# Loading the SSD's skip weights as whole rows instead of single strided values

## The chip, the cores and the metric

The kernel runs on one core of a Trainium2 chip. The metric is the time of one execution on the device in microseconds (us), and smaller is better.

## The reference, cut to what matters

The kernel computes one layer of a diffusion backbone on 512 latent tokens and 256 context tokens of width 1024: an input projection, two mixing branches (RWKV-7 and Mamba-2 SSD), a merge, and an expert-choice mixture of experts. The change concerns one small parameter of the SSD branch, `ssm_d`, with one value for each of its 32 heads. It weighs the skip path, in which a head's input is added to its output:

```python
SSM_DIM = 2 * D_MODEL        # 2048
SSM_HEAD = 64                # channels of a head
SSM_HEADS = SSM_DIM // SSM_HEAD     # 32

def ssm_readout(y, q, p):
    b_, n = y.shape[:2]
    y = (y + p['ssm_d'].astype(F32)[:, None] * q['x'].astype(F32)).reshape(b_, n, SSM_DIM)
    return rms_norm(y * jax.nn.silu(q['z'].astype(F32)), p['ssm_norm'])
```

The 2048 channels are held in 16 blocks of 128, so a block of 128 partitions holds two heads: the even one in partitions 0 to 63 and the odd one in partitions 64 to 127.

## The kernel before, in words

The kernel holds one program order for each engine. TensorE's order is written out by hand in nearly all stages (`manual_schedule`); in the stage of the change the orders of VectorE, ScalarE, GpSimd and the DMA-issuing queues are laid out at build time by a planner (`schedule_with_timeline_sim`), which estimates when each instruction is due. At run time each engine works strictly in its order.

The stages are: norms and the first projections (to 110 us), preparation of the RWKV scan woven with projections, the scan itself (from some 690 to 1100 us, four head groups `p`), the SSD (to some 1530 us), merge, routing, and the experts.

In the scan, `scan` runs twelve steps for each `p`, each a short chain of small matmuls (line 902) and copies out of PSUM: into `R` (line 930), into `SV` by VectorE (944) and by ScalarE (945), and a product (954). Between the steps `feed` lets TensorE work through blocks of the input projection (lines 312 and 315). Such a block needs its weights: a load `wraw` of 0.5 MB on SyncE's queue (line 281), a rounding `whi` on ScalarE (284), and the rest `wlo` on GpSimd (287). Its result is copied out by ScalarE into `u` (453, 454), goes through a convolution on VectorE and ScalarE (459 to 466), and GpSimd's queue stores it (468, 469). Two more things run beside the scan: the late modulation weights, with loads `adaw` of 1 MB each on SyncE's queue (157) and short rows `aext` (1549, 1550), and the scan's own loads `sAL`, `sTT`, `sBT`, `sRT`, `sRB`, `SV` of 128 to 512 KB on SyncE's queue (880 to 892).

After the scan of `p` = 1, `ssd_setup` is entered. It builds constants on VectorE (`identR`, `sel`, `neg`, lines 1011 to 1022), loads `dpar`, and computes the step sizes `dt` from a load `dt` (1034) and two loads `dtprm` (1036, 1037): the first step of that is VectorE's line 1042, then ScalarE's 1043 and 1044, and some thirty instructions on VectorE follow. Its instructions are interleaved with the scan's by the planner.

`dpar` is a tile of 128 partitions by 16: column B holds, for block B, the even head's weight in partitions 0 to 63 and the odd head's in 64 to 127. It is filled by two DMAs from GpSimd's queue (line 1025), one for each half. Each repeats one row of the source over 64 partitions (step 0) and takes 16 values with a step of two. It is read 16 times, in `ssd_out` (line 1253), where VectorE computes `xk * dpar + y`.

`ssd_setup` gets the pool `sp` for what the SSD keeps (`dpar` too) and the pool `sc2`, as `p`, for what it needs for itself. `sc2` is closed at the end of the scan's stage.

Of the kernel before, what the change touches and what calls it, by code (L numbers as in the profile page):

```python
# [8 lines left out]
F32 = mybir.dt.float32  # L9
# [78 lines left out]
class Block:  # L88
# [916 lines left out]
    def ssd_setup(self, sp, p, ps):  # L1005


        nc, A = self.nc, self.A
# [12 lines left out]
                nc.vector.tensor_scalar(self.neg[:, d, c], jp, 0.0, -30000.0, op0=op, op1=OP.mult)  # L1021
        nc.vector.memset(self.ones, 1.0)
        self.dpar = sp.tile([128, 16], F32, name="dpar")
        for h in range(2):
            nc.gpsimd.dma_start(self.dpar[64 * h:64 * h + 64, :],
                                bass.AP(tensor=A["ssm_d"].tensor, offset=A["ssm_d"].offset + h, ap=[[0, 64], [2, 16]]))
        self.CH = sp.tile([128, SEQ], F32R, name="CH")
        self.ecumT = sp.tile([128, 4, 64], F32, name="ecumT")
        self.dtT = sp.tile([128, 4, 64], F32, name="dtT")
# [1076 lines left out]
```

## Time and profile before

| | us |
|---|---|
| median of 3 runs | 2210.12 |
| lowest and highest run | 2207.89, 2210.43 |
| profiled execution, its own time | 2214.4 |
| profiled execution, its span | 2212.3 |

The busy shares over the span are 87% for TensorE's matmuls, 53% for VectorE, 38% for ScalarE and 29% for GpSimd. The HBM traffic is 222 GB/s over the span.

Times in the rows are microseconds from the span's start, unless marked ns. PE is TensorE, PEld its weight loads, DVE VectorE, ACT ScalarE, POOL GpSimd, SP SyncE; a q behind an engine's name means its queue of DMA issues. `L1025` is line 1025 of the kernel, and `out<-in` are the program's names. What stands in square brackets behind an instruction is the idle time of its engine just before it and what ended that. The granted TensorE clock (PEclk) is a share of full speed.

### The profile page before, as it was taken

How to read it: one execution, taken by the hardware profiler on the slowest of the kernel's cores; microseconds unless marked ns; L12 is line 12 of the kernel's file. 1: busy time of each engine (PE TensorE's matmuls, PEld its weight loads, DVE VectorE, ACT ScalarE, POOL GpSimd, SP SyncE). 2: the span in 40 equal slices, each digit the busy share in tenths (PEclk: the TensorE clock that was granted, in tenths of full speed). 3: DMA queues.
4: the chain of work that ended last, by engine and by line, in shares of the span. 5: the costliest groups of instructions: out<-in, count | busy, mean ns of one | idle time of the engine just before them, and what ended most of it. 6: DMA issues, size and time to landing. Idle time of an engine off the chain costs nothing. (4 is left out here: it accounts for less than half of the span.)

```text
span 2212.3 us, 35294 instructions
## 1 busy us (share of the span) xinstructions
PE 1929.1 (87%) x13996; PEld 1276.1 (58%) x14016; DVE 1176.1 (53%) x1939; ACT 846.7 (38%) x1422; POOL 631.3 (29%) x484
## 2 busy tenths in 40 slices
PE   4979888798868857999997999789999998999997
PEld 2756666566646645666675666457888453433332
DVE  4355987887894829444443466674355112322214
ACT  5444554555443323343445345444334222111113
POOL 2244342523242222232333475664211000000002
PEclk8989988989988989999999999899999998999999
DMA  6246668767889686977555344336857898999997
GB/s 233 74 116 145 164 158 192 151 173 158 193 180 240 187 170 185 292 253 218 164 157 175 99 152 140 106 133 209 300 201 274 333 366 317 409 409 409 409 409 301
DMA packets 444655, 495.15 MB, mean 224 GB/s; under 512 B 138441, under 2 KB 339391, under 8 KB 441419
## 3 DMA queue, kind: packets, MB, share of 16 engines
q1 hardware_dynamic: 419755, 449.27, 64.2%
q0 software_dynamic: 7872, 26.75, 4.2%
q10 hardware_dynamic: 16864, 16.88, 2.4%
q8 instruction: 110, 1.80, 0.3%
q14 instruction: 54, 0.44, 0.1%
HBM read 393.95 MB, written 97.98 MB: 222 GB/s over the span
## 5 line engine op out<-in xcount | busy, mean ns | idle before, releaser
L287 POOL TENSOR_TENSOR wlo<-wraw,whi 128x1024 fp32r<-128x1024 f32 x92 | 231.4, 2515 | 505.1 <-ACT whi L284 205.9
L312 PE MATMUL pl<-hlH,whi 128*128 128x512 f32 x672 | 242.2, 438 | 17.8 <-DVE hlH L257 5.9
L312 PE MATMUL pl<-hlH,wlo 128*128 128x512 f32 x672 | 239.8, 435 | 0.0
L312 PE MATMUL pl<-hlL,whi 128*128 128x512 f32 x672 | 233.7, 428 | 0.0
L1703 PE MATMUL ph<-ew,xe 128*64 128x512 f32 x432 | 196.0, 596 | 0.8 <-DMA ew<-in_exp_w_dram 0.8
L1702 PE MATMUL ph<-ew,xe 128*64 128x512 f32 x432 | 195.5, 596 | 0.0
L284 ACT ACTIVATE whi<-wraw 128x1024 fp32r<-128x1024 f32 x93 | 98.1, 1055 | 243.7 <-DMA wraw<-in_w_in_dram 160.4
L312 PEld LDWEIGHTS pl<-hlH,whi 128*128 128x128 f32 x672 | 130.0, 198 | 61.5 <-issue 15.5
L312 PEld LDWEIGHTS pl<-hlH,wlo 128*128 128x128 f32 x672 | 129.0, 198 | 38.9 <-issue 14.1
L312 PEld LDWEIGHTS pl<-hlL,whi 128*128 128x128 f32 x672 | 127.6, 195 | 39.9 <-issue 14.2
L1702 PEld LDWEIGHTS ph<-ew,xe 128*64 128x64 f32 x432 | 56.5, 137 | 109.0 <-issue 107.5
L463 DVE SCALAR_TENSOR_TENSOR cacc<-u,cst,cacc 128x772 f32<-128x772 f32 (+1 forms) x96 | 98.4, 1025 | 33.3 <-ACT cacc L459 31.7
L315 PE MATMUL pc<-hcH,whi 128*128 128x256 f32 (+1 forms) x312 | 97.1, 312 | 20.0 <-ACT u L454 14.6
L1789 PE MATMUL pye<-ew,ewx 128*64 128x512 f32 x448 | 109.9, 642 | 0.0
L315 PE MATMUL pc<-hcL,whi 128*128 128x256 f32 (+1 forms) x312 | 95.9, 311 | 0.0
L315 PE MATMUL pc<-hcH,wlo 128*128 128x256 f32 (+1 forms) x312 | 94.9, 307 | 0.0
L1212 ACT ACTIVATE M<-sel,ncumT 128x128 f32<-128x128 f32 x256 | 69.3, 387 | 67.0 <-PE sel L1209 66.9
L1709 ACT ACTIVATE ewx<-ph 128x512 f32<-128x512 f32 x30 | 17.9, 598 | 184.3 <-PE ph L1703 171.6
L1817 DVE TENSOR_TENSOR macc<-macc,psc 128x512 f32<-128x512 f32 x56 | 37.7, 685 | 89.9 <-PE psc L1812 89.8
L1213 DVE TENSOR_TENSOR M<-M,cb 128x512 f32<-128x512 f32 x64 | 63.4, 999 | 35.0 <-ACT M L1212 34.8
L466 POOL TENSOR_TENSOR cacc<-cacc,csg 128x772 f32<-128x772 f32 (+1 forms) x24 | 42.4, 1765 | 135.2 <-ACT csg L465 134.6
L315 PEld LDWEIGHTS pc<-hcH,whi 128*128 128x128 f32 (+1 forms) x312 | 61.6, 197 | 30.2 <-ACT u L454 17.8
(574 smaller groups left out, 4228.2 us busy)
## 6 DMA issues: line engine op xcount, KB each, us to landing
ew<-in_exp_w_dram SPq DMA_DIRECT2D x126, 1024.0 KB, 16.6
ew<-in_exp_w_dram SPq DMA_DIRECT2D x90, 512.0 KB, 13.1
wraw<-in_w_in_dram SPq DMA_DIRECT2D x83, 512.0 KB, 4.1
adaw<-in_ada_w_dram SPq DMA_DIRECT2D x24, 1024.0 KB, 13.7
cst<-in_exp_w_dram SPq DMA_DIRECT2D x14, 1024.0 KB, 18.0
BTd<-BT ACTq DMA_DIRECT2D x48, 256.0 KB, 4.0
sAL<-ALd SPq DMA_DIRECT2D x23, 512.0 KB, 3.8
sBT<-BTd SPq DMA_DIRECT2D x23, 512.0 KB, 6.2
```

The source lines that it names most:

```text
L284: pin(nc.scalar.activation(hi, raw, AF.Copy))
L287: self.lo.tensor_sub(lo, raw, hi.bitcast(F32))
L312: nc.tensor.matmul(pl[:n], w_[:, kt, :n], x[0][:, kt, :], **e)
L315: nc.tensor.matmul(pc[:n], w_[:, kt, :n], x[1][:, kt, :], **e)
L463: e.scalar_tensor_tensor(acc[:, s0:s0 + n0], u[:, s0 + k:s0 + k + n0], cw[:, b, k:k + 1], acc[:, s0:s0 + n0], op0=OP.mult, op1=OP.add)
L466: nc.gpsimd.tensor_mul(acc[:, s:s + n], acc[:, s:s + n], sg[:, s:s + n])
L1212: nc.scalar.activation(M[:, c], pt[:, c * 128:c * 128 + 128], AF.Exp, bias=self.ncumT[:, c, r:r + 1])
L1213: nc.vector.tensor_mul(M.rearrange("p c t -> p (c t)"), M.rearrange("p c t -> p (c t)"), cb)
L1702: nc.tensor.matmul(ph[e][f][0:64], x, w1[j][:, fs], start=kt == 0, stop=kt == 7, skip_group_check=True)
L1703: nc.tensor.matmul(ph[e][f][64:128], x, w3[j][:, fs], start=kt == 0, stop=kt == 7, skip_group_check=True)
L1789: nc.tensor.matmul(py[64 * c:64 * c + 64], hd[e][:, kt], w2[j][:, 512 * c:512 * c + 512], start=kt == 0, stop=kt == 7, skip_group_check=True)
L1817: nc.vector.tensor_add(a, a, pc)
```

## The change

The two DMAs on GpSimd's queue go. In their place one DMA on SyncE's queue loads the whole row of 32 weights into each of the 128 partitions of a new tile `dall` (the source row is repeated with a step of 0, and each partition gets 32 neighbouring values, 128 bytes). Two VectorE copies then pick the even columns for partitions 0 to 63 and the odd columns for partitions 64 to 127 into `dpar`. `dall` takes 128 bytes of each partition in the pool `sc2`.

```diff
         self.dpar = sp.tile([128, 16], F32, name="dpar")
+
+        dall = p.tile([128, 32], F32, name="dall")
+        nc.sync.dma_start(dall, bass.AP(tensor=A["ssm_d"].tensor, offset=A["ssm_d"].offset, ap=[[0, 128], [1, 32]]))
         for h in range(2):
-            nc.gpsimd.dma_start(self.dpar[64 * h:64 * h + 64, :],
-                                bass.AP(tensor=A["ssm_d"].tensor, offset=A["ssm_d"].offset + h, ap=[[0, 64], [2, 16]]))
+            nc.vector.tensor_copy(self.dpar[64 * h:64 * h + 64, :], dall[64 * h:64 * h + 64, h::2])
         self.CH = sp.tile([128, SEQ], F32R, name="CH")
```

## Rows read from the trace of the kernel before

**Rows 1.** The page: TensorE's busy tenths in 40 equal slices of the span.

```profile
PE   4979888798868857999997999789999998999997
```

**Rows 2.** Stretches: length, busy us (instructions) of each engine, granted clock, DMA share, GB/s.

```profile
799.50:812.30 12.80, 0.00 (x0) 0.00 (x0) 0.00 (x0) 0.00 (x0) 0.00 (x0) 0.69 0.88 75
...
825.00:832.00 7.00, 7.00 (x60) 5.48 (x61) 6.96 (x7) 1.27 (x3) 0.28 (x1) 0.52 0.56 159
```

**Rows 3.** The tile `dpar`: durations ns min/median/max, first and last start; time to landing.

```profile
L1253 DVE SCALAR_TENSOR_TENSOR y<-xk,dpar,sy x16: 734/748/749, 1275.3 to 1520.2; 128x512 f32<-128x512 f32 x16
L1025 POOL DMA_DIRECT2D dpar<-in_ssm_d_dram x2: 829/846/864, 786.6 to 787.5; - x2
...
DMA to landing us min/median/max: 14.6/19.7/24.9
```

**Rows 4.** DMA, 789 to 793 us: flow in 40 slices; GpSimd's queue: packets, MB, share.

```profile
GB/s 328 492 246 573 164 246 573 410 246 328 655 328 328 655 118 77 533 241 256 282 348 274 251 207 184 120 56 41 54 46 38 20 8 0 0 0 0 0 0 0
...
q0 software_dynamic: 16, 0.00, 204.4%
```

**Rows 5.** DMA, 799 to 803 us: GpSimd's queue, columns as above.

```profile
q0 software_dynamic: 29, 0.00, 233.1%
```

**Rows 6.** Stretches of 2 us, columns as in rows 2.

```profile
788.00:790.00 2.00, 1.52 (x9) 1.07 (x8) 2.00 (x10) 0.00 (x0) 0.31 (x1) 1.00 0.95 363
...
796.00:798.00 2.00, 2.00 (x25) 1.54 (x24) 0.36 (x1) 0.00 (x0) 0.79 (x2) 1.00 0.00 0
...
808.00:810.00 2.00, 0.00 (x0) 0.00 (x0) 0.00 (x0) 0.00 (x0) 0.00 (x0) 0.50 0.11 41
810.00:812.00 2.00, 0.00 (x0) 0.00 (x0) 0.00 (x0) 0.00 (x0) 0.00 (x0) 0.50 0.76 302
812.00:814.00 2.00, 0.18 (x4) 0.18 (x6) 0.00 (x0) 1.44 (x2) 0.00 (x0) 0.50 1.01 403
814.00:816.00 2.00, 2.00 (x31) 1.88 (x32) 0.00 (x0) 0.00 (x0) 0.00 (x0) 0.50 0.98 353
```

**Rows 7.** Order of time: start, duration, engine, line, instruction, idle before.

```profile
797.64 0.42 DVE L944 COPY SV<-pch 64x256 f32<-64x256 f32 x1 [2.84 <-PE pch L902]
...
812.31 1.06 ACT L284 ACTIVATE whi<-wraw 128x1024 fp32r<-128x1024 f32 x1 [18.94 <-DMA wraw<-in_w_in_dram]
...
813.82 1.01 PE L902 MATMUL pch<-SV,sBT 128*64 128x64 f32 x13 [14.36 <-ACT SV L945]
...
820.19 0.61 DVE L1042 TENSOR_SCALAR dt<-dt,dtprm 64x768 f32<-64x768 f32 x1 [22.13 <-DMA dtprm<-in_ssm_dt_bias_dram]
...
825.00 0.58 PE L315 MATMUL pc<-hcH,whi 128*128 128x256 f32 x1 [6.99 <-ACT u L454]
```

**Rows 8.** Order of time, SyncE's queue of DMA issues.

```profile
796.84 4.87 SPq L1550 DMA_DIRECT2D aext<-in_norm_post_dram  x1
812.22 0.48 SPq L1034 DMA_DIRECT2D dt<-dtd  x1
815.38 0.51 SPq L1036 DMA_DIRECT2D dtprm<-in_ssm_dt_bias_dram  x1
```

**Rows 9.** The tile `aext`: durations ns min/median/max, first and last start.

```profile
L1550 SPq DMA_DIRECT2D aext<-in_norm_post_dram x4: 227/242/4867, 796.8 to 1027.1; - x4
```

**Rows 10.** TensorE's waits, 825 to 1160 us: total, times, longest.

```profile
PE pch L902 <- DVE SV L954: 6.4, 2, 5.9
```

**Rows 11.** DMA issues of the whole span: count, KB each, median us to landing.

```profile
adaw<-in_ada_w_dram SPq DMA_DIRECT2D x24, 1024.0 KB, 13.7
...
stage<-in_rw_w_dram SPq DMA_DIRECT2D x1, 8.0 KB, 3.3
...
stage<-in_ssm_norm_dram SPq DMA_DIRECT2D x1, 8.0 KB, 1.6
```

**Rows 12.** The tile `dtend`: a copy of strided columns, durations as in rows 3.

```profile
L1081 DVE COPY dtend<-dt x1: 158/158/158, 871.0 to 871.0; 32x4 f32<-32x4 f32 x1
```

**Rows 13.** SyncE's waits ahead of its DMA issues, whole span: total, times, longest.

```profile
SPq L281 <- POOL wlo L287: 179.7, 46, 15.4
```

## The prediction

> **What bounds the kernel now.** I began with the page's row of TensorE digits, in 40 slices of 55.3 us [rows 1]. The fifteenth digit, the slice from 774 to 830 us, is a 5; between the two neighbours, 8 and 7, it is the lowest since the opening slice. Cut into stretches, that slice shows something sharper than a slow stage: from 799.5 to 812.3 us none of the five engines starts or runs a single instruction, and the DMA engines, called 88% busy there, move 75 GB/s [rows 2]. So here no engine bounds the kernel. Some transfer does, and it is not one that moves bytes.
>
> The change touches two transfers that are in flight just then: the two loads of `dpar`, issued by GpSimd at 786.6 and 787.5 us. Their first reader runs at 1275.3 us, so by themselves they may take as long as they like, and they landed after 14.6 and 24.9 us [rows 3]: 787.5 + 14.6 = 802.1 or 786.6 + 24.9 = 811.5 us for the last one, which is the end of the dead time. What they do to others is in the DMA view. GpSimd's queue starts 16 packets between 789 and 793 us, one for each DMA engine, and their time is 204.4% of the 16 engines' 4 us, which is 8.2 us for each packet [rows 4]. The next 16 start between 799 and 803 us, with 233.1% of 4 us, 9.3 us each (the other 13 packets of that row are too small to matter) [rows 5]. A load of 4 KB over 16 engines is 256 bytes or 64 values of four bytes for each engine, so a value costs 128 to 146 ns. While such a packet runs, its engine moves nothing for the other queues: the flow falls under 100 GB/s at 791.6 us and to zero at 792.4 [rows 4], is zero at 796 to 798 us, and is back to 302 GB/s only at 810 to 812 us [rows 6]. Two blocks of 8.2 and 9.3 us, from 791.6 to some 811 us, are the jam.
>
> Who waited for it is in the order of time [rows 7]: ScalarE's split of a weight block waited 18.94 us for `wraw`; behind it in ScalarE's order stood the scan's copy into SV; behind that TensorE waited 14.36 us. SyncE's queue filled too, with an issue of 4.87 us [rows 8] by a line whose median is 0.242 [rows 9], and its next two, `dt` and `dtprm`, left only at 812.22 and 815.38 us [rows 8]. VectorE therefore began the dt arithmetic at 820.19 us, after 22.13 us of waiting, and ScalarE, which stands behind that for one step, kept TensorE waiting a second time, 6.99 us until 825.00 [rows 7].
>
> **The change part by part.** Removed: two GpSimd issues of 829 to 864 ns, 1.7 us together [rows 3]. GpSimd is busy 0.31 of the 2 us that follow [rows 6], and no wait of this stretch ends on it, so that alone is worth nothing. Removed with them: 2 x 1024 four-byte writes, the jam.
>
> What the removal of the jam gives, step by step. (a) Bytes that were still queued when it began are the ones that flowed from its end until SyncE could issue `dtprm` at 815.38 us, which had waited for a modulation weight block (`adaw`): 41 x 2 + 302 x 2 + 403 x 2 + 353 x 1.4, or 1.99 MB [rows 6]. At 353 to 403 GB/s they need 4.9 to 5.6 us. Without the jam they run from 791.6 us and are done at about 797. (b) `dtprm` then goes out at 797 instead of 815.38 us, and VectorE starts the dt step 4.81 us later, as before (815.38 to 820.19) [rows 7, 8]: at 802.0, which is 18.2 us earlier. (c) `wraw` is part of the same 1.99 MB and lands before 797 us, so ScalarE's split is done when VectorE's SV copy at 797.64 us [rows 7] has run, and the 14.36 us on TensorE go. (d) TensorE's second wait ends 4.81 us after VectorE's dt step starts (820.19 to 825.00), so at 806.8, again 18.2 us earlier. Both engines that set the pace afterwards are shifted by the same 18.2 us, and I take that as the worth of the jam.
>
> Is it kept to the end? From 799.5 to 812.3 us everything stood still, so no engine used the time to get ahead, and nothing later starts by an outside clock. TensorE's longest wait up to 1160 us, after the one of 6.99, is 5.9 us, on VectorE [rows 10]: a queue of work behind an engine that is itself shifted, and no place where 18 us of slack would swallow the gain.
>
> The clock adds nothing to the sum. After the two stalls TensorE ran at a granted 0.52 (the level of 1.2 GHz, not 2.4) from 825 to 832 us, 7.00 us busy, some 3.4 us more than at full clock; but VectorE was 6.96 us busy in the same 7 us [rows 2], so it sets that stretch. The 3.4 us stay as an upper end.
>
> Added: (1) one SyncE issue of 128 rows of 128 bytes. The nearest are SyncE's small parameter loads of 8 KB in rows of 512 bytes, landing in 1.6 and 3.3 us [rows 11]; the upper bound charges each of the 8 rows per engine like a four-byte value, 8 x 146 = 1.2 us. It is likelier near the first, since no row among the others costs 146 ns. Its issue, 0.23 us for the quickest `aext` load [rows 9] up to 0.5 for `dt` [rows 8], stands ahead of `dt`, `dtprm` and the scan's next loads on SyncE's queue, but those wait for `wraw` and `adaw` anyway, which covers it; uncovered it is 0.5 us. (2) Two VectorE copies of 64x16 with a step of two: a copy of 32x4 out of strided columns took 158 ns [rows 12], the scan's copy into SV, 64x256, 0.42 us [rows 7]; two are 0.3 to 0.85 us. VectorE had 2.84 us idle just ahead of the SV copy [rows 7], which hides them. (3) A new wait: the copies wait for the load, and VectorE works in order, so what stands behind them waits too. The load goes out after the `aext` pair, or about when that would leave an unjammed queue (790 to 792 us), behind the 1.99 MB on the same rings; it lands at about 797 to 798. If the copies stand where VectorE was idle, behind the SV copy of 797.64 us, this costs nothing; if they stand directly behind the `neg` instructions at 790 us, ahead of the scan's copy there, it costs up to 8 us. I take zero, because the copies follow the `neg` lines only in the text and VectorE's order here is laid out by due times, and keep 8 for the range.
>
> The Trainium skill ("DMA: Bandwidth & Descriptors", section "Measured (HBM→SBUF, 128 partitions, SWDGE, issued from GpSimd)") has 4 KB loaded through GpSimd's queue at 0.68 us of DMA time; by that figure the two loads would hold the engines for 1.4 us instead of 17.5, the jam would have another cause, and the change would be worth nothing. This trace disagrees with it for values of four bytes, by 8.2 and 9.3 us for the same 4 KB.
>
> **Sum.** 18.2 us off. Against the profiled execution: 2214.4 - 18.2 = 2196.2 us. That execution was 4.3 us over the median of the timed runs, so against the median: 2210.1 - 18.2 = 2191.9, rounded to 2192 us. The ends: at least the 12.8 us in which all stood still (2197.3), at most the whole jam from 791.6 to 811.8 us plus the clock's 3.4, 23.6 us (2186.5).
>
> **Rivals.** *A, VectorE waits for the new load.* The copies are ordered ahead of the scan's copy at 790 us; 8 of the 18.2 us come back: 2200. For it: the new load shares SyncE's rings with 2 MB. Against: VectorE is busy 2.00 of 2.00 us from 788 to 790 [rows 6] and idle soon after, and an order by due times has those later, emptier places.
> *B, slower.* The load is held on SyncE's queue behind an issue that waits for a buffer, while the copies already stand at VectorE's head, in front of the scan. The longest such wait of a weight load is 15.4 us [rows 13]; with 4.81 us to landing it is 20.2 us, 2.0 more than the gain: 2212 at the median's level. With a few such microseconds more it would be slower by over 0.2%. It decides only if the load is issued after 812 us, and the waits seen ahead of `dt` were themselves made by the jam, so I give it little.
> *C, the jam is not theirs.* The packets' length could be a result of a blockade by the 1 MB `adaw` loads rather than its cause; then the change does nothing and the time stays near 2209. Against it: the 24 `adaw` loads have a median of 13.7 us to landing [rows 11], less than the jam alone; and the flow falls exactly when the 16 packets start and rises when the second 16 end. The rule quoted above belongs here.
> *D, more than the sum.* VectorE's dense stretch also shortens, since TensorE at full clock feeds it earlier: 22 to 24 us, 2187.
>
> **How the numbers follow.** Main case, 2189 to 2197: 0.68. D: 0.09. A and other part givings-back, 2197 to 2204: 0.14. C: 0.04. B: 0.05. The range takes in the main case, D and A: 2185 to 2202. A measurement of this kernel tells about 0.2%, 4.4 us, from no change; faster by more than that are the main case, D and nearly all of A, 0.90; the rest of A with C is within, 0.05; slower 0.05.
>
> **What would show it.** In the profile after, the stretch from 792 to 812 us should hold matmuls throughout, with no zero in the flow of the DMA; GpSimd's queue should have no packets longer than 1 us there; `wraw`'s wait at the same split should shrink from 18.94 to under 3 us, `dtprm` should leave SyncE near 797 and the dt step start near 802 us. The step (a) fails if the flow after 792 us is far below 350 GB/s; the kept part fails if events at 1275 us (the first use of `dpar`) are shifted by much less than 18 us. The forecast is wrong altogether if the zero flow stays, or if VectorE shows a wait for `dall` of over 8 us.

## The result, and the profile after

The changed kernel took 2183.82 us (median of 4 runs, 2174.01 to 2186.15) beside 2209.01 us for the kernel before (2204.41 to 2210.43). The ratio is 0.9898 with a 95% interval of 0.9864 to 0.9932, so 22.5 us less, with 15.0 to 30.0 us inside the interval; the two medians alone are 25.2 us apart, and the text goes by the ratio. The forecast was 18.2 us less, 2192 us in a range of 2185 to 2202. The change is the one forecast; the median lies a little beyond the range's fast end. The profiled execution of the changed kernel took 2184.98 us.

TensorE's digits in 40 slices, on the page of the changed kernel (the line of rows 1):

```profile
PE   4979798889768887999997999789999998999997
```

The fifteenth digit is an 8 where it was a 5. The stretches of rows 2 (length, busy us and instructions of PE, PEld, DVE, ACT and POOL, granted clock, DMA share, GB/s), with the one in which the jam would have begun ahead of them:

```profile
784.00:799.00 15.00, 12.18 (x161) 9.51 (x163) 5.06 (x12) 4.71 (x7) 5.40 (x6) 1.00 1.04 319
799.50:812.30 12.80, 10.74 (x122) 7.97 (x118) 11.90 (x13) 6.34 (x10) 0.03 (x1) 1.00 0.66 195
825.00:832.00 7.00, 6.06 (x49) 3.75 (x50) 6.91 (x10) 2.43 (x3) 1.47 (x1) 1.00 0.73 245
```

Where nothing ran from 799.5 to 812.3 us, TensorE is now busy for 10.74 of 12.80 us at full clock, and the DMA engines move 319 GB/s just before. One sign that the forecast named came out otherwise: the flow is still zero for a moment.

```profile
806.00:807.50 1.50, 1.50 (x20) 1.29 (x15) 1.50 (x1) 1.09 (x2) 0.00 (x0) 1.00 0.00 0
```

The DMA share is 0.00 there too, and TensorE is busy all the time: nothing is being moved, and nothing is jammed. The changed kernel reached this stage some 6 us earlier: GpSimd's `ncumT` instruction, the last one before the point of the change, started at 780.42 us, and at 786.44 in the kernel before. The instruction orders of the two kernels are the same up to there, so those 6 us are no work of the change, and I measure below from that instruction on.

SyncE's queue in order of time (start, duration of the issue, line, transfer; rows 8 are the counterpart; the lines after the change have numbers higher by two):

```profile
783.38 0.47 SPq L891 DMA_DIRECT2D sRT<-RTd  x1
...
785.16 0.26 SPq L1552 DMA_DIRECT2D aext<-in_norm_post_dram  x1
786.88 0.36 SPq L1026 DMA_DIRECT2D dall<-in_ssm_d_dram  x1
789.38 0.48 SPq L1036 DMA_DIRECT2D dt<-dtd  x1
791.35 0.39 SPq L887 DMA_DIRECT2D sBT<-BTd  x1
791.85 1.32 SPq L880 DMA_DIRECT2D SV<-VTd  x2
793.26 0.56 SPq L892 DMA_DIRECT2D sRB<-RBd  x1
793.86 0.50 SPq L1038 DMA_DIRECT2D dtprm<-in_ssm_dt_bias_dram  x1
```

The issue of `aext` that took 4.87 us takes 0.26, and `dtprm` leaves at 793.86 us. The engines in order of time (the counterpart of rows 7):

```profile
790.32 1.06 ACT L284 ACTIVATE whi<-wraw 128x1024 fp32r<-128x1024 f32 x1 [3.11 <-PE pc L315]
...
793.50 0.35 DVE L1028 COPY dpar<-dall 64x16 f32<-64x16 f32 x2 [4.86 <-DMA dall<-in_ssm_d_dram]
793.98 0.42 DVE L944 COPY SV<-pch 64x256 f32<-64x256 f32 x1
...
794.45 1.03 PE L902 MATMUL pch<-SV,sBT 128*64 128x64 f32 x15 [1.42 <-DVE SV L944]
...
796.94 1.11 ACT L454 ACTIVATE u<-pl 128x512 f32<-128x512 f32 x1 [2.13 <-PE pl L312]
...
798.10 0.38 PE L315 MATMUL pc<-hcH,whi 128*128 128x256 f32 x1 [0.84 <-ACT u L454]
...
800.07 0.61 DVE L1044 TENSOR_SCALAR dt<-dt,dtprm 64x768 f32<-64x768 f32 x1 [3.61 <-DMA dtprm<-in_ssm_dt_bias_dram]
...
801.34 0.83 ACT L1045 ACTIVATE dt<-dt 64x768 f32<-64x768 f32 x1
```

ScalarE's split no longer waits for `wraw`; its 3.11 us are put down to TensorE. TensorE's two waits of 14.36 and 6.99 us have become 1.42 and 0.84. One wait is new: VectorE stands 4.86 us for `dall`, with the scan's SV copy right behind.

### The profile page after: what moved, and what is told of

Same layout as the page of the kernel before. It is cut to its first block, busy times and chain, and to the rows that moved or that the text cites. A ratio compares the mean times of both kernels' runs of the same rounds, so it can differ in the third digit from the quotient of the medians.

```text
span 2183.1 us, 35294 instructions
## 1 busy us (share of the span) xinstructions
PE 1923.5 (88%) x13996; PEld 1270.6 (58%) x14016; DVE 1171.0 (54%) x1941; ACT 847.5 (39%) x1423; POOL 634.0 (29%) x482
## 5 line engine op out<-in xcount | busy, mean ns | idle before, releaser
L1870 POOL TENSOR_TENSOR macc<-macc,x 128x512 f32<-128x512 f32 x7 | 11.4, 1653 | 227.8 <-DVE macc L1869 226.5
```

## The experiments

All medians stand beside runs of the kernel before on the same chip. In the table, "stage" is the time from the start of GpSimd's `ncumT` instruction to the start of the first instruction that reads `dpar` (rows 3 for the kernel before), both from the profile of each kernel. It leaves out what differs before the change's place and after the first use. Each stage is one profiled execution; e5_x_same, which still has the jam, stands 3.0 us from the kernel before, so differences of that size say nothing.

| kernel | median us | before, us | ratio, 95% interval | `ncumT` | first use | stage, us | against before |
|---|---|---|---|---|---|---|---|
| before | | | | 786.4 | 1275.3 | 488.9 | |
| changed | 2183.82 | 2209.01 | 0.9898 (0.9864 to 0.9932) | 780.4 | 1249.6 | 469.2 | -19.7 |
| e1_rows64 | 2190.37 | 2210.72 | 0.989 (0.9871 to 0.991) | 786.3 | 1259.9 | 473.6 | -15.3 |
| e2_pairs | 2198.80 | 2210.72 | 0.9943 (0.9918 to 0.9967) | 786.8 | 1269.3 | 482.5 | -6.4 |
| e3_spread | 2198.37 | 2210.72 | 0.9937 (0.992 to 0.9955) | 781.4 | 1256.1 | 474.7 | -14.2 |
| e4_sp_single | 2200.17 | 2210.72 | 0.9966 (0.9941 to 0.9991) | 783.5 | 1267.7 | 484.2 | -4.7 |
| e5_x_same | 2205.13 | 2209.31 | 0.999 (0.997 to 1.0009) | 773.3 | 1265.2 | 491.9 | +3.0 |
| e6_adjacent | 2193.22 | 2209.31 | 0.9929 (0.9907 to 0.9951) | 778.7 | 1252.9 | 474.2 | -14.7 |
| e7_early | 2187.92 | 2209.31 | 0.9904 (0.9881 to 0.9927) | 786.1 | 1256.0 | 469.9 | -19.0 |
| e8_none | 2187.53 | 2209.31 | 0.9907 (0.9877 to 0.9937) | 781.5 | 1252.1 | 470.6 | -18.3 |

**Runs instead of single values, all else as before (e1_rows64).**

```diff
-  ... offset=A["ssm_d"].offset + h, ap=[[0, 64], [2, 16]]))
+  ... offset=A["ssm_d"].offset + 16 * h, ap=[[0, 64], [1, 16]]))
```

> The kernel before with one thing changed: each of the two loads on GpSimd's queue takes 16 neighbouring values for a partition (one run of 64 bytes) instead of 16 single ones with a step of two. Queue, number of loads, bytes and the instruction order of every engine stay as before. It puts the weights of other heads into dpar. Theory 1 (a single value costs 128 to 146 ns of a DMA engine, and the 64 of a packet block the other queues): packets of at most 1 us, no stretch without flow between 786 and 812 us, TensorE's wait of 14.36 us gone, 18 to 22 us faster, about 2187 to 2191. Rival (the new order of the engines' instructions gave the gain, or any load on GpSimd's queue at this place blocks): the dead time stays, 2205 to 2210.

This is the cleanest run of the study: no engine's order differs from the kernel before. It took 0.989 of the time, as much as the changed kernel. GpSimd's packets between 789 and 793 us (queue: packets, MB, share of 16 engines' time):

```profile
q0 software_dynamic: 64, 0.01, 20.7%
```

All 64 together hold the engines for 20.7% of 4 us, 0.83 us for each engine, where 16 of them held them for 8.2 us [rows 4]. And the steps of the forecast can be read off in a kernel with the old order: first the stretch in which the queued bytes flow (columns as above), then SyncE, ScalarE's split, VectorE and TensorE:

```profile
791.60:797.00 5.40, 5.40 (x73) 4.25 (x70) 1.74 (x4) 1.69 (x2) 3.57 (x5) 1.00 1.00 347
```

```profile
797.02 0.50 SPq L1036 DMA_DIRECT2D dtprm<-in_ssm_dt_bias_dram  x1
```

```profile
796.16 1.06 ACT L284 ACTIVATE whi<-wraw 128x1024 fp32r<-128x1024 f32 x1 [3.11 <-PE pc L315]
```

```profile
802.52 1.39 DVE L1042 TENSOR_SCALAR dt<-dt,dtprm 64x768 f32<-64x768 f32 x1 [4.79 <-DMA dtprm<-in_ssm_dt_bias_dram]
```

```profile
808.11 0.58 PE L315 MATMUL pc<-hcH,whi 128*128 128x256 f32 x1 [6.86 <-ACT u L454]
```

The forecast had 797, 802.0 and 806.8 us for SyncE, VectorE and TensorE. The split no longer waits for `wraw`. The rival in which the new order of instructions made the gain is out, and so is the one in which any load on GpSimd's queue jams.

**Half as many runs, the same bytes (e2_pairs).**

```diff
-  nc.gpsimd.dma_start(self.dpar[64 * h:64 * h + 64, :], ... ap=[[0, 64], [2, 16]]))
+  nc.gpsimd.dma_start(self.dpar[64 * h:64 * h + 64, :].rearrange("p (i j) -> p i j", j=2), ... ap=[[0, 64], [4, 8], [1, 2]]))
```

> The kernel before with the same two loads in runs of two neighbouring values (8 bytes): half as many runs, the same bytes. It puts the weights of other heads into dpar. Theory 1 (the price is for each run): packets of 4.1 to 4.7 us instead of 8.2 and 9.3, a jam of about 9 us instead of 17.5, and a time about half way, 2198 to 2202. Rival (the price is for bytes or for the load as a whole): packets of 8 to 9 us and no change, 2205 to 2210.

GpSimd's queue from 790 to 793 us and from 793 to 798.5 us:

```profile
q0 software_dynamic: 16, 0.00, 118.9%
```

```profile
q0 software_dynamic: 33, 0.00, 90.0%
```

118.9% of 3 us is 3.6 us for each of the first 16 packets, and 90.0% of 5.5 us is 4.95 us for each engine after that. Together 8.5 us instead of 17.5: half the reads, half the jam, and about half the gain (6.4 of 15.3 us in the stage). The bytes are the same, so bytes are not what is paid for.

**Single values, but each partition from a row of its own (e3_spread), and the control (e5_x_same).**

```diff
-  tensor=A["ssm_d"].tensor, offset=A["ssm_d"].offset + h, ap=[[0, 64], [2, 16]]
+  tensor=A["x"].tensor, offset=A["x"].offset + 65536 * h, ap=[[1024, 64], [2, 16]]     # e3_spread
+  tensor=A["x"].tensor, offset=A["x"].offset + 65536 * h, ap=[[0, 64], [2, 16]]        # e5_x_same
```

> The kernel before with the same two loads of 64x16 single values with a step of two, but each partition reads from a row of its own of x (rows 4 KB apart) instead of all 64 from the same 128 bytes of ssm_d. dpar holds values of x. Theory 1 (the single values are what is slow): packets of 8 to 9.5 us as before, no change, 2203 to 2211. Rival (64 partitions that read one and the same address are what is slow): packets of under 3 us and most of the 18 to 22 us gained, below 2195.

> Control for the run with spread rows: the kernel before, its two loads of 64x16 single values read from x, but again all 64 partitions from one and the same 128 bytes. dpar holds values of x. Theory 2 (many reads of one address are served one after another, some 8 to 9 ns each, 1024 of them for a load): packets of 8 to 9.5 us and the dead time are back, 2203 to 2213. Rival (the place of the small tensor ssm_d is slow, or the reads are fast from any other tensor): packets of about 2.6 us as with spread rows, 2190 to 2200.

Here the first theory fell. e3_spread still moves 1024 single values with a step of two in each load, with every engine's order as before, and yet 14.2 us of the stage are gone. GpSimd's queue in e3_spread from 786 to 788 us, in which the first load's packets start, and from 789 to 791 us:

```profile
q0 software_dynamic: 30, 0.01, 81.9%
```

```profile
q0 software_dynamic: 19, 0.00, 7.3%
```

81.9% of 2 us is 1.6 us for each engine, after which the packets are hardly to be seen. The time missed the rival's "below 2195": 2198.37 us, a ratio of 0.9937 (0.992 to 0.9955), is clearly less of a gain than e1's 0.989 (0.9871 to 0.991) on the same chip, though the profiled stages of the two are only 1.1 us apart. What single values from distant rows still cost in the timed runs stays open. The control reads the same tensor x at one address again, and the jam is back: the queue from 776 to 780 us, and the stretches (columns as above):

```profile
q0 software_dynamic: 16, 0.00, 209.9%
```

```profile
778.00:787.00 9.00, 8.27 (x109) 6.55 (x107) 2.91 (x6) 0.85 (x1) 3.61 (x5) 1.00 1.00 19
787.00:799.00 12.00, 0.00 (x0) 0.00 (x0) 0.00 (x0) 0.00 (x0) 0.00 (x0) 0.60 0.83 119
```

16 packets of 209.9% of 4 us are 8.4 us each, 12 us in which no engine runs, and a ratio of 0.999. So what makes the jam is not the single value, and not where `ssm_d` lies. It is that all 64 partitions, over all 16 DMA engines, read one and the same 128 bytes.

The control's second load, which reads another 128 bytes than the first, tells one thing more. Its first packet alone, from 786.57 to 786.60 us, and GpSimd's queue from 786.5 to 787.5 and from 787.5 to 789 us:

```profile
q0 software_dynamic: 1, 0.00, 16.9%
```

```profile
q0 software_dynamic: 19, 0.00, 2.9%
```

```profile
q0 software_dynamic: 17, 0.01, 401.1%
```

16.9% of 16 x 0.03 us is 0.08 us. By the records of the single packets, four of the load's 16 packets start before 787.5 us, one after another, and take 0.08 us each; the other twelve start from 787.5 to 788.8 us and take 1.2 to 10.6 us, for the same 64 reads of the same block. So an engine does not pay a fixed price for each read of a shared address by itself; in this load engines were slow when many read the block at the same time.

**Single values from neighbouring blocks (e6_adjacent).**

```diff
+  tensor=A["x"].tensor, offset=A["x"].offset + 65536 * h, ap=[[32, 64], [2, 16]]
```

> As the run with spread rows, but the 64 partitions read 64 neighbouring blocks of 128 bytes of x (8 KB in one piece) instead of rows 4 KB apart. dpar holds values of x. Theory 2 (it is the same address that counts): packets of 2 to 3 us, 2190 to 2200. Rival (any small region of memory is slow): packets of 6 us or more, above 2200.

GpSimd's queue from 783 to 787 us, which holds both loads:

```profile
q0 software_dynamic: 63, 0.01, 4.6%
```

4.6% of 16 x 4 us is 2.9 us for 63 packets. If all of it belonged to the 32 of the two loads, one would take 0.09 us on average; with reads at one address it takes 8.2 to 9.3. The 0.09 us is far below the 2 to 3 us expected; the time, 2193.22 us, is as expected. A small region of memory is therefore not slow by itself, and 64 single values with a step of two cost next to nothing when the partitions read from different blocks.

**The same loads on SyncE's queue (e4_sp_single).**

```diff
-            nc.gpsimd.dma_start(self.dpar[64 * h:64 * h + 64, :],
+            nc.sync.dma_start(self.dpar[64 * h:64 * h + 64, :],
```

> The kernel before with the same two loads of single values issued on SyncE's queue instead of GpSimd's. Theory 1 (single values are slow on whichever queue): the 128 values for each engine block SyncE's own ring for 13 to 18 us, whatever stands behind them on that ring waits, and the time stays at 2203 to 2213. Rival (it is GpSimd's queue, whose packets are long, that blocks): no stretch without flow, 15 to 20 us faster, 2189 to 2195.

Stretches (columns as above), and ScalarE's split and TensorE's next wait in order of time:

```profile
786.00:794.00 8.00, 7.03 (x93) 5.44 (x93) 4.58 (x10) 1.81 (x3) 3.56 (x5) 1.00 1.04 373
794.00:811.00 17.00, 7.71 (x104) 5.95 (x102) 1.26 (x3) 3.45 (x5) 2.36 (x1) 0.88 0.16 41
```

```profile
793.42 1.06 ACT L284 ACTIVATE whi<-wraw 128x1024 fp32r<-128x1024 f32 x1 [3.09 <-PE pc L315]
```

```profile
821.70 1.12 PE L902 MATMUL pch<-R,sTT 64*64 64x64 f32 x16 [19.14 <-DVE R L930]
```

The flow falls to 41 GB/s for 17 us here as well, 8.3 ns for each of the 2048 reads, so GpSimd's queue is not what makes the reads slow. The DMA engines look different, though: their share is 0.16, where it was 0.88. GpSimd's and SyncE's queues from 796 to 806 us:

```profile
q0 software_dynamic: 128, 0.39, 9.7%
q1 hardware_dynamic: 1073, 0.00, 4.8%
```

SyncE's 1073 packets in 10 us are one every 9.3 ns over all 16 engines together, and 4.8% of 16 x 10 us is 7.2 ns for each. No packet holds an engine for long here, and GpSimd's stores still move 0.39 MB; what waits stands behind the reads on SyncE's own queue. The time came out below what I expected all the same, 2200 us, and the stage is 4.7 us shorter than before. On SyncE's queue the two loads stand behind `wraw`, which had landed in time: the split at 793.42 us waited for TensorE and not for a transfer. So the first wait, of 14.36 us, is not there. What stands behind the reads on the queue, `dt` and `dtprm`, is held instead, VectorE waits for it with the scan's next copy behind, and TensorE has one wait of 19.14 us in place of 14.36 and 6.99. The planner laid out VectorE's and ScalarE's orders anew in this kernel, so its time mixes the two.

**The row load early (e7_early), and no load at all (e8_none).**

```diff
 # e7_early: in the stage's setup, at about 690 us
+  B.dall = sc.tile([128, 32], F32, name="dall")
+  tc.nc.sync.dma_start(B.dall, bass.AP(tensor=A["ssm_d"].tensor, offset=A["ssm_d"].offset, ap=[[0, 128], [1, 32]]))
 # e8_none: in place of both loads
+  nc.vector.memset(self.dpar, 1.0)
```

> The changed kernel with the row load of 32 values issued early, at the start of the scan's stage (about 690 us), so that VectorE's two copies find it landed. The order of the engines' instructions is laid out anew after it. Theory: VectorE's wait of 4.86 us for dall is gone; TensorE gets back the 2 to 3 us that this wait cost the scan: 2181 to 2187 where the changed kernel has 2184 to 2190. Rival (the wait is hidden by projection work): no difference beyond 2 us.

> No load of the skip weights at all: dpar is set to one by VectorE. The skip weights are left out of the computation. It gives the most that can be had from this load. Theory: within 3 us of the changed kernel with the early load, 2181 to 2188, and TensorE without a wait over 8 us between 785 and 815 us. Rival (the changed kernel's row load still costs something): 2175 to 2180.

VectorE in e7_early, in order of time:

```profile
787.33 0.29 DVE L1027 COPY dpar<-dall 64x16 f32<-64x16 f32 x2
...
790.03 0.41 DVE L944 COPY SV<-pch 64x256 f32<-64x256 f32 x1
```

The wait of 4.86 us is gone, and nothing is won: 0.9904 beside the changed kernel's 0.9898, and 19.0 beside 19.7 us in the stage. The 2181 to 2187 us of the theory was missed by a little, with 2187.92. In the changed kernel TensorE has matmuls of the projection to do for most of VectorE's wait and stands still for 1.42 us at its end. But e7 changes a second thing: its traces show the orders of the kernel before on SyncE and nearly so on ScalarE and VectorE, and with them TensorE's wait for `u` is back:

```profile
PE pc L315 <- ACT u L454: 3.6, 1, 3.6
```

So e7 shows that the early load is worth nothing in all, and not the price of VectorE's wait by itself. e8_none, without any load, is no faster either; its orders are those of the kernel before on every engine. As far as an interval of some 7 us either way can tell, the change has won all there was to win on this load.

## Why the prediction was right, and where it was not

*The jam belongs to the two `dpar` loads.* Right. Changing nothing but which values they read takes the dead time away (e1, e3, e6) or leaves it (e5). Rival C is out.

*What a packet costs, and why.* The mechanism was wrong. The forecast divided 8.2 and 9.3 us by 64 values and called 128 to 146 ns the price of a single value. e6_adjacent moves the same single values at no more than 0.09 us for a packet on average. The price is for a read of an address that other engines read at the same time: 1024 reads in 8.2 to 9.3 us are 8.0 to 9.1 ns each, if all 16 engines are served in series; e2 with 512 reads gives 7.0 and 9.7 ns, e5 8.2 ns and e4 8.3 ns. That they are in series is argued from the pace in e4, where one packet comes every 9.3 ns over all engines, and from the unequal packets of e5's second load. The forecast could not tell the two apart, since the loads of before have both properties, and its size did not hang on it. Its upper bound for the new load, 8 rows of 146 ns, was a figure of the wrong kind: 128 reads of the shared row at 8 to 9 ns would be about 1.1 us, and e8_none shows no cost to the kernel that the runs can tell.

The Trainium skill ("DMA: Bandwidth & Descriptors", section "Measured (HBM→SBUF, 128 partitions, SWDGE, issued from GpSimd)") has 4 KB at 0.68 us. The forecast held the trace against it as a matter of four-byte values. That was too wide: with single values from different blocks (e6) a packet takes no more than 0.09 us on average, and only reads of a shared address, which the section does not speak of, take 8.2 us and more.

*Steps (a) to (d).* Right to within 1.4 us where the order of instructions stayed as it was: 797.02, 802.52 and 808.11 us in e1 for a forecast of 797, 802.0 and 806.8. The bytes of step (a) check as well: 347 GB/s from 791.6 to 797.0 us are 1.87 MB, for 1.99 forecast. In the changed kernel the same path was built differently. Counted from the `ncumT` instruction, `dtprm` leaves at 13.4 us (28.9 before, 10.7 in e1), because SyncE's new order puts four of the scan's loads (`sBT`, two of `SV`, `sRB`) ahead of it, and the dt step starts at 19.7 us (33.8 before, 16.3 in e1). That would have been a smaller gain than 18.2 us. But ScalarE's new order also puts its copy to `u` ahead of the dt step, so TensorE no longer stands behind `dtprm` at all: its wait of 6.99 us is 0.84, where e1 with the old order still has 6.86. In the kernel before, ScalarE had the dt step first:

```profile
820.83 0.84 ACT L1043 ACTIVATE dt<-dt 64x768 f32<-64x768 f32 x1 [7.06 <-DVE dt L1042]
...
823.85 1.09 ACT L454 ACTIVATE u<-pl 128x512 f32<-128x512 f32 x1
```

The stage became 19.7 us shorter, against 15.3 in e1, and 18.2 by the sum; the sum met the total and not this split. The nearest test of the sum is e8_none, with the old order and no load: 18.3 us, so the new order was not needed for the gain, though a scatter of 3 us can't tell 15.3 from 18.3.

*Kept to the end.* Right. The first use of `dpar` moved by 25.7 us, 19.7 without the head start, and the span by 29.2, 23.2 without it.

*Rival A, a wait for `dall`.* It came, in half: the copies stand ahead of the scan's SV copy, but at its later turn, and VectorE waits 4.86 us and not up to 8. I had priced such a wait at its full length on the path. It cost less: in the kernel before, the same copy had 2.84 us of idle time ahead of it already, for TensorE, so the wait put it off by some 2.5 us, and TensorE, which had other work, stood 1.42 us. In the total e7 shows no price, but with other orders.

*The clock.* Not shown. In the kernel before TensorE ran at 0.52 from 825 to 832 us [rows 2], after standing still. The same work stands in e1 from 808 to 815 us:

```profile
808.00:815.00 7.00, 6.89 (x60) 5.38 (x61) 6.96 (x6) 1.38 (x4) 0.17 (x1) 0.51 0.53 153
```

The clock is as low behind the one wait of 6.86 us, and VectorE is as busy, so e1 does not price it. In the changed kernel the clock is 1.00 in every stretch shown above, but other work stands in them. That VectorE sets the stretch fits, but no run changes the clock alone.

*The size.* The sum was 18.2 us, measured were 22.5 (15.0 to 30.0); e1, whose order is that of before, has 24.3 (19.9 to 28.5). The profiles place 15 to 20 us of it in the stage. What the rest is stays open: the same instructions ahead of the stage took between 773.3 and 786.8 us in the profiles of the table, more than the difference to be explained, and what follows the first use of `dpar` took between 933.5 and 939.2 us.

## What to carry to other kernels

A load that repeats a small source over many partitions should read each row as one run, so that few reads go to the shared address; the step in the source is not what made the jam. Look for stretches in which all engines stand still and the DMA share is high but the flow is near zero: here a few long packets held the DMA engines (0.88 and 75 GB/s), and a transfer that nobody waits for stopped everyone. With the same reads on SyncE's queue the share was low as well (0.16), and what stood behind them on that queue was stopped. To price such a load, vary which addresses it reads and keep its shape, since the order of all engines then stays as it was.

## What the runs showed of the hardware

I had not expected that reads of one address by many DMA engines cost 7 to 10 ns each over all engines, as if they went one after another, whichever queue issues them. Nor had I expected that a packet of 64 single values with a step of two takes under 0.1 us on average when the partitions read neighbouring blocks (e6); from rows 4 KB apart (e3) the first load still took 1.6 us for each engine. On GpSimd's queue a packet of reads of a shared address held its DMA engine for 8.2 to 9.3 us, and the other queues moved nothing meanwhile; on SyncE's queue (e4) no packet held an engine, and GpSimd's queue went on. The second load of e5 suggests that several engines at once are what it takes: packets that read the block one after another took 0.08 us. Whether they then collide over the same address, the same 128 bytes or a larger piece of the memory was not tried apart.
